# First four experts gathered with the selection matrix stationary, the second-block group moved into mid-stream, stores on two queues

## The chip, the cores and the metric

The kernel runs on one core of a Trainium2 chip. The metric is the device time of one execution in microseconds (us). The unchanged kernel takes 2122.4 us (median of 3 runs, 2119.12 to 2123.26). The core has five engines that run side by side: PE (TensorE, matrix products), DVE (VectorE), ACT (ScalarE), POOL (GpSimd) and SP (SyncE, which here issues most DMAs). In the rows, PEld is PE's loading of the stationary operand.

## The reference, cut to what matters

The program is one layer of one network block and one layer of another, over 512 tokens of width 1024. Nothing is changed in the first three quarters of it. The change is in the last part, a mixture of 64 experts, with two experts for each token:

```python
g_sel = argmax(h2 @ w_rg + b_rg)                  # one of 8 groups of experts
top_v, top_i = top_k(e_logits, 2)                 # two of the 8 experts of that group
gate = p_group * softmax(top_v)
def expert_block(xb, e):
    hid = silu(xb @ w_gate_e[e]) * (xb @ w_up_e[e])     # 1024 -> 256
    return hid @ w_down_e[e]                            # 256 -> 1024
return x + sum over a token's experts of gate * expert_block(h2[token], e)
```

Here `h2` is the normalised sum `x`. Each expert has three float32 matrices of 1 MB, so the weights of the 64 experts are 192 loads of 1 MB.

## The kernel before, in words

**Groups.** Every expert gets a block of 32 slots for tokens, and four experts form a group of 128 slots. `N_Q` is 15: groups 0 to 14 hold four experts each, and group 15 (`H` in the code) holds experts 60 and 61, in 64 slots. Group 16 (`L`) holds the two spare places, experts 62 and 63, each with a first and a *second* block: four blocks of 32 slots for two experts' weights. An expert with more tokens than its slots is put at one of these spare places: `order_prep`, run in groups 1 and 2, permutes the experts from number 24 on, so from there on the load of a weight reads the expert's number from a register (`value_load` in `pump_w`). What is still left over is done in a loop at the very end, whose trip count `nov` is read from memory; the profiled execution doesn't enter it.

**Routing and the first gather** (`ev_out2`, m = 3). The 512 tokens are four tiles of 128 (`m`). For the last tile PE does the transposes of x, the router's logits, and between them the gather of group 0's tokens. That gather is a matrix product with the selection matrix S (`moe["q"][0][1]`, 128 tokens x 128 slots, already scaled by each token's norm): in `gather_quick` the rows of x are the stationary operand, read with a stride of eight columns, and S is streamed, eight products of 128 columns per tile into two PSUM banks, opened by a product with a zero tile (`gather_open`). The result stands transposed (model width on the partitions), so that `gather_last` needs only to scale it by `g8` while it copies it out.

**The order behind it.** DVE picks the two experts per token (`choose`), PE ranks the tokens (`rank`), DVE builds S, PE does the last tile of the gather. Then come `gather_last`, the slots, the index table and the indirect fetch of group 1, the first pair of experts (`pair(0, 0, 0)`), the second pair, the rest of the gates and tables, and `second(0)`.

**A group.** `pair(Q, j, e)` is 32 products (gate and up of two experts, four at a time in column quarters); the trace shows each float32 product as two records, so a pair is 64 records. Between the pairs stand the table and fetch of the next group (`ready`) and the additions of the group before to x (`combine`, products in float32r, then an add on DVE for each half tile). `second` is `hidden`, the 16 products of `down` (32 records), and `group_out`, which splits the result into a high and a low part on ACT and DVE. `turn` transposes the fetched tokens of the next group.

**The weight stream.** `w_order` lists the 192 loads. `pump_w` issues them on SP's queue, in that order, as long as fewer than `N_LIVE` = 13 are live. A load counts as live until the product that uses it is over (`drop_w` in `pair` and `second`). Expert 3 (`E_SMALL`) is loaded in halves into other buffers and isn't counted. `pair(..., last=False)` doesn't drop, so that the spare experts' gate and up serve two pairs.

**The end.** After group 14 come L (its two pairs directly after one another), then H: PE adds x's tiles 1 and 3 into four PSUM banks with an identity product (`sums`, float32), and adds H's result there; tiles 0 and 2 are added on DVE. Eight stores of half a tile go out on SP, in the order of the tiles. Then `nov` is loaded on all engines, the loop is passed over, and the program ends with a DRAIN on each engine.

The lines: L1534 to L1597 `ev_out2` and its tail, L2007 and L2008 `gather_last`, L1857 the weight loads, L113 every product (`mm`), L2292 to L2301 the end, L2366 the end of the program.

Of the kernel before, what the change touches and what calls it, by code (L numbers as in the profile page):

```python
# [12 lines left out]
BF16 = mybir.dt.bfloat16  # L13
# [7 lines left out]
P = 128  # L21
# [57 lines left out]
def layer_kernel(ctx, tc, A, out, dbg=None, stop=None):  # L79
# [1430 lines left out]
    def ev_out2(m, pss):  # L1510
        last = m == NM - 1
        xap = nxt["x"][m]
        xh = halves(xap)
        hT = []

        def tr(b, on_act):
            ps = bank((P, 4, P), "h2T")
            for k in range(4):
                pe.transpose(ps[:, k, :], xap[:, (4 * b + k) * P:(4 * b + k + 1) * P], ident)
            t = m2((P, 4, P), name="h2T")  # L1520
            (act.activation(t, ps, AF.Copy) if on_act else dve.tensor_copy(t, ps))
            hT.append(t)

        def logits():
            lp = bank((P, 96), "lg")
            for k in range(8):
                mm(lp, hT[k // 4][:, k % 4, :], wr[:, k, :], start=k == 0, stop=k == 7)
            return lp

        def biased(lp):  # L1530
            dve.scalar_tensor_tensor(L[:, m, :], lp[:, 0:72], rs_[:, m:m + 1], ro["rbias"], op0=ALU.mult, op1=ALU.add)

        for x_, p_ in zip(xh, pss):
            dve.tensor_tensor(x_, x_, p_, op=ALU.add)  # L1534
        gp.dma_start(x_d[2][m * P:(m + 1) * P, :], xap)
        parts = []

        def rstd_chain(squares):
            return rstd_steps(xh, parts, squares) + [
                lambda: dve.tensor_tensor(rs_[:, m:m + 1], parts[0], parts[1], op=ALU.mult)]  # L1540

        squares = sum_squares(xh)
        if not last:
            steps = rstd_chain(squares)
            if m == 2:
                alternate(steps, rank(0, 2))
            else:
                alternate(steps)
            later(2, lambda: (tr(0, True), tr(1, True)))

            def choice():
                biased(logits())
                if m:
                    alternate(choose(0 if m == 1 else m, m + 1))
            later(3, choice)
            return
        gather_open()
        gather_quick(0, (0, 1))
        tr(0, True)
        tr(1, False)  # L1560
        rk2 = rank(m - 1, m)
        gather_quick(1, (0,))
        lp = logits()
        gather_quick(1, (1,))
        alternate(rstd_chain(squares), rk2)
        gather_quick(2, (0, 1))
        biased(lp)
        alternate(choose(m, m + 1))
        gate_exps()
        alternate(rank(m, m + 1))  # L1570
        gather_quick(3, (0, 1))

    def strided(t, k):

        return t.rearrange("p (i k) -> p k i", k=8)[:, k, :]

    def gather_open():

        moe["gz"] = m2(dt=BF16, name="zero")
        gp.memset(moe["gz"], 0.0)  # L1580
        moe["gps"] = [bank((P, 4, P), "xqT") for _ in range(2)]
        for ps in moe["gps"]:
            mm(ps.rearrange("p k s -> p (k s)"), trb[:, 1, :], moe["gz"], start=True, stop=False)

    def gather_quick(m, bs):

        for b in bs:
            for k in range(4):
                mm(moe["gps"][b][:, k, :], strided(nxt["x"][m], 4 * b + k), moe["q"][0][1][:, m, :],
                   start=False, stop=m == NM - 1 and k == 3)  # L1590

    def gate_exps():

# [270 lines left out]

    N_Q = N_EXP // 4 - 1

    E_SMALL, N_FIRST, N_LIVE = 3, 10, 13
    w_order = []  # L1870
    for e in [*range(0, 4 * N_Q, 2), N_EXP - 2, N_EXP - 4]:
        w_order += [(e + j, i) for j in range(2) for i in range(2)]
        if e >= 4 * N_Q:
            w_order += [(e + j, 2) for j in range(2)]
        elif e % 4:
            w_order += [(e - 2 + j, 2) for j in range(4)]
# [125 lines left out]

    def gather_last():

        xT[0] = [m2((P, 4, P), name="xqT") for _ in range(2)]
        for k in range(4):
            act.activation(xT[0][0][:, k, :], moe["gps"][0][:, k, :], AF.Copy, scale=g8[:, k:k + 1])  # L2007
        dve.tensor_tensor(xT[0][1], moe["gps"][1], g8[:, 4:8, None].to_broadcast([P, 4, P]), op=ALU.mult)  # L2008


    def gate_up(xcs, wts):
# [62 lines left out]
        mm(ps, sel, RkT[0])  # L2074
        dve.tensor_scalar(STs[Q], ps, C("pmod"), None, op0=ALU.is_equal)  # L2075

    def add_group(ps, Q, m, h, start):

        for i, t in enumerate(ys[Q]):
            if Q == N_Q:  # L2080
                r = slice(64 * h, 64 * h + 64)
                mm(ps, STs[Q][r, m * P:(m + 1) * P], t[r, 0], start=start and i == 0, stop=i == 1)
            else:
                mm(ps, STs[Q][:, m * P:(m + 1) * P], t[:, h], start=start and i == 0, stop=i == 1)

    def combine(Q, ms):

# [116 lines left out]
        dve.tensor_copy(ov["key"], p3)  # L2204

    gt_ = gating()
    next(gt_)
    gather_last()
    group_tokens()
    slots(1)  # L2210
    table(1, 4, 6)
    fetch(1)
    for _ in gt_:
        pass
    group_gates()
    sel_S[0] = moe["q"][0][0]
    order, prep = order_prep(), overflow_prep()

# [22 lines left out]
        table(Q)  # L2241
        fetch(Q)

    part = [pair(0, j, j) for j in (0, 2)]
    table(0, 0, 4)
    table(1, 0, 4)
    rank_cols()
# [1 line left out]
    scatter_mat(0)  # L2249
    second(0, hids, range(4))  # L2250
    turn(1)
    for Q in range(1, N_Q):
        part = pair(Q, 0, 4 * Q)
        ready(Q + 1 if Q < N_Q - 1 else Q + 2)
        if Q == N_Q - 2:
            ready(N_Q)
        combine(Q - 1, range(2))
        hids = [hidden(part)]
        part = pair(Q, 2, 4 * Q + 2)
        if Q in (1, 2):  # L2260
            next(order, None)
            next(order, None)
        if Q in (8, 9, 10, 11):
            next(prep, None)
        combine(Q - 1, range(2, NM))
        scatter_mat(Q)
        hids.append(hidden(part))
        turn(Q + 1 if Q < N_Q - 1 else Q + 2)
        second(Q, hids, range(4 * Q, 4 * Q + 4))
    L, H, e = N_Q + 1, N_Q, N_EXP - N_SPARE  # L2270
    part = [pair(L, j, e, last=j > 0) for j in (0, 2)]
    combine(L - 2, range(NM))
    hids = [hidden(p_) for p_ in part]
    scatter_mat(L)
    turn(H)
    second(L, hids, [e, e + 1, e, e + 1])
    scatter_mat(H)
    combine(L, range(NM))

    part = pair(H, 0, 4 * H)  # L2280
    sums = {m: [bank(name="cmb") for _ in range(2)] for m in (1, 3)}
    for m in sums:
        for ps, x_ in zip(sums[m], halves(xt[m])):
            mm(ps, ident, x_, start=True, stop=False)
    hids = [hidden(part)]
    second(H, hids, [4 * H, 4 * H + 1])
    assert wnext["i"] == len(w_order) and not ew and next(order, None) is None and next(prep, None) is None
    for m in range(NM):
        for h, x_ in enumerate(halves(xt[m])):
            if m in sums:  # L2290
                add_group(sums[m][h], H, m, h, False)
                act.activation(x_, sums[m][h], AF.Copy)  # L2292
            else:
                ps = bank(name="cmb")
                add_group(ps, H, m, h, True)
                dve.tensor_tensor(x_, x_, ps, op=ALU.add)
            sp.dma_start(out[0, m * P:(m + 1) * P, h * T:(h + 1) * T], x_)


    nov = nc.values_load(ov["n"][0:1, 0:1], min_val=0, max_val=MAXBLK)  # L2300
    with tc.For_i(0, nov, 1):  # L2301
        ev = sp.value_load(ov["e"][0:1, 0:1], min_val=0, max_val=N_EXP - 1)
        wts = [load_w(i, ev) for i in range(3)]
# [66 lines left out]
```

## Time and profile before

| | |
|---|---|
| median of 3 runs | 2122.4 us (2119.12 to 2123.26) |
| the profiled execution | 2125.34 us, span in the trace 2123.5 us |
| PE busy | 1969.9 us, 93% of the span |
| DVE / ACT / POOL busy | 1127.8 / 752.2 / 103.6 us |
| granted PE clock, mean | 0.959 of full speed |
| HBM read / written | 363.20 MB / 11.10 MB |

In a timeline a row is start, length, engine, line, operation, what it writes and reads, how many records are merged, and in brackets the engine's idle time before it and what ended it. PE's busy time says little here: its matmuls overlap, and their ends are modelled. What matters is which wait ends last, and what the DMA engines move: in the page's 40 slices their rate is 407 to 420 GB/s in slices 32 to 39, the expert part, and far lower before.

### The profile page before, as it was taken

To read this page: it belongs to the slowest core of one execution; us is meant where nothing else is said; L and a number is where in the kernel's file an instruction comes from. 1 tells how busy PE (TensorE), PEld (TensorE's weight loads), DVE (VectorE), ACT (ScalarE), POOL (GpSimd) and SP (SyncE) were. 2 spreads that over 40 slices of the span, in tenths; PEclk is the share of its full clock that TensorE was granted. 3 is DMA by queue.
4 is the path that set the end of the run, shared out by engine and by line. 5 is a ranking of instruction groups with operands and counts; after the bars stand their busy time and mean duration, and the time that the engine had idled before them with its cause. 6 is when DMAs were issued, how large, how long until landed. Compare 5 with 4: busy or idle time off the path is not lost. (4 is left out here: it accounts for less than half of the span.)

```text
span 2123.5 us, 28581 instructions
## 1 busy us (share of the span) xinstructions
PE 1969.9 (93%) x11228; PEld 1480.0 (70%) x11228; DVE 1127.8 (53%) x2447; ACT 752.2 (35%) x1460; POOL 103.6 (5%) x119
## 2 busy tenths in 40 slices
PE   7999999999999999999999999999998887768775
PEld 6777788888888888775678888888876444335433
DVE  5444536436756532878765787766443433343333
ACT  5443323325544422534542654653221211111111
POOL 3000000001000000121110000000000000000000
PEclk9999999999999999999999999999998888888888
DMA  9522222254222262301123332334367999999992
GB/s 223 198 89 68 82 89 72 89 198 139 73 67 80 70 225 92 122 21 28 54 70 109 114 97 90 100 99 119 122 237 274 407 419 419 420 419 420 419 412 115
DMA packets 167193, 369.45 MB, mean 174 GB/s; under 512 B 19033, under 2 KB 117665, under 8 KB 142864
## 3 DMA queue, kind: packets, MB, share of 16 engines
q1 hardware_dynamic: 157536, 341.31, 43.5%
q0 software_dynamic: 9520, 26.28, 4.2%
q8 instruction: 90, 1.47, 0.3%
q14 instruction: 47, 0.39, 0.1%
HBM read 363.20 MB, written 11.10 MB: 176 GB/s over the span
## 5 line engine op out<-in xcount | busy, mean ns | idle before, releaser
L113 PE MATMUL ws<-hTh,wh 128*128 128x512 f32 x1152 | 468.4, 407 | 0.3 <-ACT q2T L1072 0.3
L113 PE MATMUL ws<-hTh,wl 128*128 128x512 f32 x1152 | 450.0, 391 | 0.0
L113 PE MATMUL ws<-hTl,wh 128*128 128x512 f32 x1152 | 449.8, 390 | 0.0
L345 DVE TENSOR_TENSOR wl<-raw,wh 128x1024 fp32r<-128x1024 f32 x230 | 283.9, 1235 | 308.9 <-ACT wh L338 308.1
L338 ACT ACTIVATE wh<-raw 128x1024 fp32r<-128x1024 f32 x247 | 259.0, 1052 | 233.3 <-PE ws L113 106.5
L113 PEld LDWEIGHTS ws<-hTh,wh 128*128 128x128 f32 x1152 | 216.6, 188 | 63.1 <-issue 18.6
L113 PEld LDWEIGHTS ws<-hTh,wl 128*128 128x128 f32 x1152 | 216.6, 188 | 47.0
L113 PEld LDWEIGHTS ws<-hTl,wh 128*128 128x128 f32 x1152 | 217.0, 188 | 43.1 <-issue 2.2
L113 PE MATMUL gu<-we,xT 128*32 128x256 f32 x1984 | 157.5, 434 | 44.7 <-DMA we<-in_w_up_e 30.4
L690 DVE SCALAR_TENSOR_TENSOR cv<-ws,pcol,cv 128x510 f32<-128x510 f32 (+1 forms) x152 | 113.8, 749 | 115.7 <-ACT cv L688 112.5
L113 PEld LDWEIGHTS gu<-we,xT 128*32 128x32 f32 x1984 | 74.7, 124 | 125.8 <-DMA we<-in_w_up_e 42.2
L2092 DVE TENSOR_TENSOR x<-x,cmb 128x512 f32<-128x512 f32 x128 | 79.6, 682 | 60.1 <-PE cmb L113 59.0
L688 ACT ACTIVATE cv<-ws,pcol 128x512 f32<-128x512 f32 x64 | 49.7, 776 | 108.5 <-PE ws L113 108.5
L2018 ACT ACTIVATE part<-gu 128x256 f32<-128x256 f32 x33 | 12.7, 384 | 201.6 <-PE gu L113 201.6
L113 PE MATMUL down<-we,hid 128*32 128x512 f32 x528 | 74.8, 716 | 1.0 <-DVE hid L2031 1.0
L113 PE MATMUL cmb<-ys,ST 128*128 128x512 f32 (+1 forms) x272 | 71.9, 415 | 1.2 <-ACT ys L2055 0.9
L113 PE MATMUL xs<-wh,hTh 128*128 128x512 f32 x160 | 65.9, 412 | 2.1 <-ACT wh L338 2.0
L113 PE MATMUL xs<-wl,hTh 128*128 128x512 f32 x160 | 64.0, 400 | 2.6 <-DVE wl L345 2.6
L2057 DVE SCALAR_TENSOR_TENSOR ys<-down,slot,ys 128x512 fp32r<-128x512 f32 x33 | 24.8, 751 | 76.4 <-ACT ys L2055 76.4
L113 PE MATMUL xs<-wh,hTl 128*128 128x512 f32 x160 | 63.8, 399 | 0.7 <-DVE hTl L307 0.7
L113 PE MATMUL full<-wh,fh 128*128 128x512 f32 x160 | 62.3, 390 | 0.0
L113 PE MATMUL full<-wl,fh 128*128 128x512 f32 x160 | 62.3, 389 | 0.0
(544 smaller groups left out, 3068.1 us busy)
## 6 DMA issues: line engine op xcount, KB each, us to landing
we<-in_w_gate_e SPq DMA_DIRECT2D x63, 1024.0 KB, 19.8
we<-in_w_up_e SPq DMA_DIRECT2D x63, 1024.0 KB, 19.9
we<-in_w_down_e SPq DMA_DIRECT2D x63, 1024.0 KB, 20.1
raw<-in_w_in SPq DMA_DIRECT2D x56, 1024.0 KB, 5.3
raw<-in_w_up SPq DMA_DIRECT2D x22, 1024.0 KB, 5.1
raw<-in_w_down SPq DMA_DIRECT2D x11, 1024.0 KB, 6.1
raw<-in_w_out SPq DMA_DIRECT2D x8, 1024.0 KB, 4.9
AC<-acum_d POOLq DMA_DIRECT2D x16, 512.0 KB, 4.9
```

The source lines that it names most:

```text
L113: pe.matmul(o, l, r, start=start, stop=stop)
L338: act.activation(hi, src, AF.Copy)
L345: eng.tensor_tensor(lo, src, hi.bitcast(F32), op=ALU.subtract)
L688: act.activation(a, src, AF.Identity, scale=taps[0], bias=bias)
L690: dve.scalar_tensor_tensor(a[:, lag:], src[:, :T - lag], taps[lag], a[:, lag:], op0=ALU.mult, op1=ALU.add)
L2018: act.activation(part, gu, AF.Copy)
L2057: dve.scalar_tensor_tensor(lo[:, h], ps, g, hi[:, h].bitcast(F32), op0=ALU.mult, op1=ALU.subtract)
L2092: dve.tensor_tensor(x_, x_, ps, op=ALU.add)
```

## The change

Five things are changed; the diff is cut to their core.

1. The first gather has S stationary and streams x (two products of 512 columns per tile in place of eight of 128). Its result stands with slots on the partitions, so `gather_last` copies it out and transposes it with eight PE transposes before the scaling. The zero tile goes.
2. The slots, table and fetch of group 1, and the rest of the gates, move behind the first pair of group 0 (table and fetch between the two pairs).
3. Group L moves from the end to the place after group 7 (`N_MID` = 8), in the order of the work and in that of the loads, and runs in the loop like any other group. The overflow steps (`prep`) come with groups 9 to 12 in place of 8 to 11.
4. After the last fetch, in group 13, POOL gets a `drain`.
5. At the end x's tiles 1 and 3 take the results of groups 14 and H in PSUM; `nov` is read before H; tiles 1 and 3 are stored whole from ACT's queue, tiles 0 and 2 in halves from SP's, in the order 1, 0, 3, 2.

```diff
-        gather_open()
-        gather_quick(0, (0, 1))
         tr(0, True)
         tr(1, False)
         rk2 = rank(m - 1, m)
-        gather_quick(1, (0,))
+        gather_quick(0)
         lp = logits()
-        gather_quick(1, (1,))
         alternate(rstd_chain(squares), rk2)
-        gather_quick(2, (0, 1))
         biased(lp)
+        gather_quick(1)
+        gather_quick(2)
         alternate(choose(m, m + 1))
         gate_exps()
         alternate(rank(m, m + 1))
-        gather_quick(3, (0, 1))
+        gather_quick(3)
...
+    def gather_quick(m):
+        if m == 0:
+            moe["gps"] = [bank(name="xq") for _ in range(2)]
+        for ps, x_ in zip(moe["gps"], halves(nxt["x"][m])):
+            mm(ps, moe["q"][0][1][:, m, :], x_, start=m == 0, stop=m == NM - 1)
...
-    for e in [*range(0, 4 * N_Q, 2), N_EXP - 2, N_EXP - 4]:
+    N_MID = 8
+    for e in [*range(0, 4 * N_MID, 2), N_EXP - 2, *range(4 * N_MID, 4 * N_Q, 2), N_EXP - 4]:
...
     def gather_last():
+        xq = [m2((P, 4, P), name="xq") for _ in range(2)]
+        for h, ps in enumerate(moe["gps"]):
+            v = ps.rearrange("p (i k) -> p k i", k=8)
+            act.activation(xq[0][:, :, 64 * h:64 * h + 64], v[:, 0:4], AF.Copy)
+            dve.tensor_copy(xq[1][:, :, 64 * h:64 * h + 64], v[:, 4:8])
         xT[0] = [m2((P, 4, P), name="xqT") for _ in range(2)]
-        for k in range(4):
-            act.activation(xT[0][0][:, k, :], moe["gps"][0][:, k, :], AF.Copy, scale=g8[:, k:k + 1])
-        dve.tensor_tensor(xT[0][1], moe["gps"][1], g8[:, 4:8, None].to_broadcast([P, 4, P]), op=ALU.mult)
+        for b in range(2):
+            ps = bank((P, 4, P), "xqT")
+            for k in range(4):
+                pe.transpose(ps[:, k, :], xq[b][:, k, :], ident)
+            if b == 0:
+                dve.tensor_tensor(xT[0][0], ps, g8[:, 0:4, None].to_broadcast([P, 4, P]), op=ALU.mult)
+            else:
+                for k in range(4):
+                    act.activation(xT[0][1][:, k, :], ps[:, k, :], AF.Copy, scale=g8[:, 4 + k:5 + k])
...
-    part = [pair(0, j, j) for j in (0, 2)]
+    part = [pair(0, 0, 0)]
+    slots(1)
+    table(1, 4, 6)
+    fetch(1)
+    part.append(pair(0, 2, 2))
+    for _ in gt_:
+        pass
+    group_gates()
...
+    L, H = N_Q + 1, N_Q
+    seq = [*range(N_MID), L, *range(N_MID, N_Q), H]
+    for i in range(1, len(seq) - 1):
+        Q = seq[i]
+        e = 4 * Q if Q < N_Q else N_EXP - N_SPARE
+        es = [e + j for j in range(4)] if Q < N_Q else [e, e + 1, e, e + 1]
+        part = pair(Q, 0, e, Q < N_Q)
+        if i < len(seq) - 3:
+            ready(seq[i + 1])
+        elif i == len(seq) - 3:
+            ready(seq[i + 1])
+            ready(H)
+            gp.drain()
+        combine(seq[i - 1], range(2))
...
-    L, H, e = N_Q + 1, N_Q, N_EXP - N_SPARE
-    part = [pair(L, j, e, last=j > 0) for j in (0, 2)]
-    combine(L - 2, range(NM))
-    hids = [hidden(p_) for p_ in part]
-    scatter_mat(L)
-    turn(H)
-    second(L, hids, [e, e + 1, e, e + 1])
     scatter_mat(H)
-    combine(L, range(NM))
-    part = pair(H, 0, 4 * H)
     sums = {m: [bank(name="cmb") for _ in range(2)] for m in (1, 3)}
     for m in sums:
         for ps, x_ in zip(sums[m], halves(xt[m])):
             mm(ps, ident, x_, start=True, stop=False)
+    combine(seq[-2], (0, 2))
+    for m in sums:
+        for h in range(2):
+            add_group(sums[m][h], seq[-2], m, h, False, False)
+    nov = nc.values_load(ov["n"][0:1, 0:1], min_val=0, max_val=MAXBLK)
+    part = pair(H, 0, 4 * H)
     hids = [hidden(part)]
     second(H, hids, [4 * H, 4 * H + 1])
-    for m in range(NM):
+    for m in (1, 0, 3, 2):
+        rows = out[0, m * P:(m + 1) * P, :]
         for h, x_ in enumerate(halves(xt[m])):
...
-            sp.dma_start(out[0, m * P:(m + 1) * P, h * T:(h + 1) * T], x_)
-    nov = nc.values_load(ov["n"][0:1, 0:1], min_val=0, max_val=MAXBLK)
+                sp.dma_start(rows[:, h * T:(h + 1) * T], x_)
+        if m in sums:
+            act.dma_start(rows, xt[m])
```

## Rows read from the trace of the kernel before

**Rows 1.** The page, chain of work that ended last, shares of the span by line.
```profile
DMA we<-in_w_up_e 12%; PE gu L113 3%; DMA we<-in_w_down_e 3%; PE cmb L113 1%; PE down L113 1%; PE xqT L113 1%; PE tab L113 0%; DVE x L2092 0%; PE xT L1995 0%; ACT xg L1990 0%; PE ST L113 0%; DVE ov L2167 0%; PE hid L2026 0%; PE lg L113 0%; DVE ST L2075 0%
```
**Rows 2.** Stretches: length, busy of PE, PEld, DVE, ACT, POOL; clock, DMA share, GB/s.
```profile
1595.00:1600.00 5.00, 4.29 (x20) 4.17 (x20) 0.00 (x0) 0.12 (x2) 0.66 (x2) 0.66 0.98 317
...
1609.00:1625.00 16.00, 13.33 (x103) 9.91 (x106) 5.03 (x18) 1.14 (x4) 1.15 (x1) 0.68 0.09 28
...
1625.00:2082.00 457.00, 358.10 (x3113) 194.86 (x3105) 164.65 (x390) 77.89 (x175) 15.05 (x16) 0.85 1.00 412
```
**Rows 3.** Weight loads: first issue after the pause; last issue (last figure), times to landing.
```profile
1624.98 0.33 SPq L1857 DMA_DIRECT2D we<-in_w_gate_e  x1
...
L1857 SPq DMA_DIRECT2D we<-in_w_down_e x4: 333/333/333, 2050.3 to 2067.7; - x4
...
DMA to landing us min/median/max: 19.2/19.7/19.9
```
**Rows 4.** Timeline of the routing of the last tile and the first gather.
```profile
1593.02 1.28 DVE L1534 TENSOR_TENSOR x<-x,full 128x512 f32<-128x512 f32 x2
...
1599.86 1.04 PE L1519 MATMUL h2T<-ca,x 128*128 128x128 f32 x8
...
1602.80 1.92 PE L113 MATMUL lg<-routing,h2T 128*128 128x96 f32 x16
...
1604.56 5.90 PE L113 MATMUL xqT<-S,x 128*128 128x128 f32 x24
...
1608.18 0.23 DVE L1630 TENSOR_TENSOR routing<-rscr,routing 128x64 bf16<-128x64 f32 x1
...
1611.78 4.18 PE L113 MATMUL xqT<-S,x 128*128 128x128 f32 x16 [1.20 <-DVE S L1649]
...
1617.43 1.84 PE L113 MATMUL tab<-routing,S 128*128 128x2 f32 x8 [1.47 <-DVE S L1956]
...
1619.19 3.21 PE L113 MATMUL gu<-we,xqT 128*32 128x256 f32 x28
```
**Rows 5.** PE's timeline of group 3, which waits for no load.
```profile
1696.84 3.63 PE L113 MATMUL gu<-we,xT 128*32 128x256 f32 x64
...
1701.31 2.10 PE L113 MATMUL cmb<-ys,ST 128*128 128x512 f32 x8
...
1720.49 0.60 PE L113 MATMUL gu<-we,xT 128*32 128x256 f32 x6
```
**Rows 6.** Timeline from group 14's second pair to the last addition.
```profile
2047.64 3.64 PE L113 MATMUL gu<-we,xT 128*32 128x256 f32 x58 [1.85 <-DMA we<-in_w_up_e]
...
2058.88 4.38 PE L113 MATMUL down<-we,hid 128*32 128x512 f32 x32
...
2082.95 3.64 PE L113 MATMUL down<-we,hid 128*32 128x512 f32 x32
...
2088.38 0.49 PE L113 MATMUL ST<-RkT,sel 64*128 64x512 f32 x1 [1.79 <-DVE sel L2072]
...
2096.25 3.70 PE L113 MATMUL cmb<-x,ca 128*128 128x512 f32 x8
...
2099.78 0.39 PE L2026 MATMUL hid<-ca,part 128*128 128x128 f32 x2
...
2101.19 1.92 PE L113 MATMUL down<-we,hid 128*32 128x512 f32 x16 [1.01 <-DVE hid L2031]
...
2105.31 2.48 DVE L2296 TENSOR_TENSOR x<-x,cmb 128x512 f32<-128x512 f32 x4 [0.59 <-PE cmb L113]
```
**Rows 7.** Stores and the program's end: durations min/median/max (ns), first and last start (us).
```profile
L2297 SPq DMA_DIRECT2D out<-x x8: 348/406/1553, 2106.0 to 2110.7; - x8
...
DMA to landing us min/median/max: 2.1/4.0/4.4
...
L2366 POOLq DRAIN  x3: 46/103/7173, 2115.5 to 2123.2; - x3
L2366 SPq DRAIN  x3: 7/7/13, 2116.6 to 2122.9; - x3
```

More of the change, by code (lines that the diff above doesn't have):

```diff
@@ L1570, in ev_out2 @@
         alternate(rank(m, m + 1))
-        gather_quick(3, (0, 1))
+        gather_quick(3)
     def strided(t, k):
         return t.rearrange("p (i k) -> p k i", k=8)[:, k, :]
[L1577 to L1587, printed above, removed]
-            for k in range(4):
-                mm(moe["gps"][b][:, k, :], strided(nxt["x"][m], 4 * b + k), moe["q"][0][1][:, m, :],
-                   start=False, stop=m == NM - 1 and k == 3)
+    def gather_quick(m):
[3 more added lines that the diff above has]
+            mm(ps, moe["q"][0][1][:, m, :], x_, start=m == 0, stop=m == NM - 1)
     def gate_exps():
@@ L2003, in gather_last @@
     def gather_last():
-        xT[0] = [m2((P, 4, P), name="xqT") for _ in range(2)]
-        for k in range(4):
-            act.activation(xT[0][0][:, k, :], moe["gps"][0][:, k, :], AF.Copy, scale=g8[:, k:k + 1])
-        dve.tensor_tensor(xT[0][1], moe["gps"][1], g8[:, 4:8, None].to_broadcast([P, 4, P]), op=ALU.mult)
+        xq = [m2((P, 4, P), name="xq") for _ in range(2)]
[3 more added lines that the diff above has]
+            dve.tensor_copy(xq[1][:, :, 64 * h:64 * h + 64], v[:, 4:8])
+        xT[0] = [m2((P, 4, P), name="xqT") for _ in range(2)]
+        for b in range(2):
[7 more added lines that the diff above has]
+                    act.activation(xT[0][1][:, k, :], ps[:, k, :], AF.Copy, scale=g8[:, 4 + k:5 + k])
     def gate_up(xcs, wts):
@@ L2075, in scatter_mat, with add_group @@
         dve.tensor_scalar(STs[Q], ps, C("pmod"), None, op0=ALU.is_equal)
-    def add_group(ps, Q, m, h, start):
+    def add_group(ps, Q, m, h, start, stop=True):
         for i, t in enumerate(ys[Q]):
@@ L2081, in add_group @@
                 r = slice(64 * h, 64 * h + 64)
-                mm(ps, STs[Q][r, m * P:(m + 1) * P], t[r, 0], start=start and i == 0, stop=i == 1)
+                mm(ps, STs[Q][r, m * P:(m + 1) * P], t[r, 0], start=start and i == 0, stop=stop and i == 1)
             else:
-                mm(ps, STs[Q][:, m * P:(m + 1) * P], t[:, h], start=start and i == 0, stop=i == 1)
+                mm(ps, STs[Q][:, m * P:(m + 1) * P], t[:, h], start=start and i == 0, stop=stop and i == 1)
     def combine(Q, ms):
@@ L2206, in layer_kernel @@
     gt_ = gating()
+    gather_last()
     next(gt_)
-    gather_last()
     group_tokens()
[L2210 to L2215, printed above, removed]
     sel_S[0] = moe["q"][0][0]
@@ L2251, in layer_kernel @@
     turn(1)
[L2252 to L2257, printed above, removed]
+    L, H = N_Q + 1, N_Q
[12 more added lines that the diff above has]
+        combine(seq[i - 1], range(2))
         hids = [hidden(part)]
-        part = pair(Q, 2, 4 * Q + 2)
+        part = pair(Q, 2, es[2])
         if Q in (1, 2):
@@ L2262, in layer_kernel @@
             next(order, None)
-        if Q in (8, 9, 10, 11):
+        if Q in (9, 10, 11, 12):
             next(prep, None)
-        combine(Q - 1, range(2, NM))
+        combine(seq[i - 1], range(2, NM))
         scatter_mat(Q)
         hids.append(hidden(part))
-        turn(Q + 1 if Q < N_Q - 1 else Q + 2)
-        second(Q, hids, range(4 * Q, 4 * Q + 4))
-    L, H, e = N_Q + 1, N_Q, N_EXP - N_SPARE
-    part = [pair(L, j, e, last=j > 0) for j in (0, 2)]
-    combine(L - 2, range(NM))
-    hids = [hidden(p_) for p_ in part]
-    scatter_mat(L)
-    turn(H)
-    second(L, hids, [e, e + 1, e, e + 1])
+        turn(seq[i + 1])
+        second(Q, hids, es)
     scatter_mat(H)
-    combine(L, range(NM))
-    part = pair(H, 0, 4 * H)
     sums = {m: [bank(name="cmb") for _ in range(2)] for m in (1, 3)}
```

## The prediction

> **What bounds the kernel now.** I read the chain of waits first. Its largest parts are loads of expert weights, we<-in_w_up_e above all; PE's own parts are small [rows 1]. So in the expert part it is the weight stream that ends last, and PE's work counts only before the stream runs and after it has ended. The windows say the same: from 1625 to 2082 the DMA share is 1.00 at 412 GB/s, but in the 16 us before it is 0.09 [rows 2]. There all 13 live buffers are full, and SP's next load goes out at 1624.98 [rows 3], when the first pair of experts, started at 1619.19, has let its weights go [rows 4]. From there 176 of the 192 loads follow each other without a break. The last is issued at 2067.7 and lands some 19.7 us later [rows 3]: the stream ends at T = 2087.4. With eight loads in flight, 19.7 us to landing is 2.46 us for a load.
>
> Three places are left in which time can be won: the way to the first pair (it shifts the stream, and with it T), the work after T (the last addition ends at 2107.8 [rows 6], 20.4 us later), and the way from there to the end at 2123.5. The sum is made on the span; the profiled execution took 2125.34 us, 2.9 above the median of 2122.4, and I take the same gain off the median.
>
> **Change 1 and 2, the first gather.** x's last tile is complete at 1594.3, the first pair starts at 1619.19 [rows 4]: 24.9 us. Now the new way. A streamed float32 product of 512 columns costs what the identity products of the end cost: 8 records in 3.70 us [rows 6], so 4 records, one tile of the gather, 1.8 us. Before, 24 records of 128 columns took 5.90 and the last 16 took 4.18 [rows 4], about 4 us for a tile. With PE at the upper of its two levels (2.4 GHz; the lower is 1.2):
> - transposes of x: 8 in 1.04 [rows 4], half of them after the second half of x, and three small rank products: to 1595.2;
> - tile 0 of the gather 1.8, logits 1.92 [rows 4]: to 1598.9, where the old logits end at 1604.7;
> - DVE's choice, unchanged, from the old logits' end to 1608.41 [rows 4], 3.7: to 1602.6. Tiles 1 and 2 of the gather (3.6) lie beneath it. Before, the rank products had to wait for the gather until 1610.46 [rows 4];
> - rank to the last S, old 1610.46 to 1611.78 [rows 4], 1.3, then the last tile 1.8: to 1605.7;
> - the new copies, estimated 0.5, four transposes 0.5, the scaling of 128x512 on DVE 0.7 (an addition of that size takes 2.48/4 = 0.6 [rows 6]), and waits 0.2: first pair at 1607.6. The other half of the copies, transposes and scalings lies beside the pair's first half.
>
> That is 11.6 us earlier. The bound below: PE's granted clock was 0.66 in 1595 to 1600 and 0.68 in 1609 to 1625 [rows 2], a mix of its two levels, after idle stretches. At the lower one two uncovered tiles cost 1.8 more each and the transposes 0.5: 7.5 us earlier. I take 10. The moved table takes 1.84 [rows 4] at most; it now stands between the two pairs, so group 0's down weights come free that much later, measured from the first issue. The six loads let go by the pairs cover 6 x 2.46 = 14.8 us and nearly that wait; I cost it 0.5, at most 1.8 if the cover is gone. The zero tile and its products go at no gain beyond this sum. **T moves from 2087.4 to 2077.9.**
>
> **Change 3, group L in mid-stream.** For T it is free if the stream doesn't run dry. A group in which PE waits for nothing takes 1720.49 - 1696.84 = 23.7 us [rows 5]. Twelve loads take 29.5, L's six 14.8, each with a token fetch on top. So in L PE falls back by some 9 us, 3.6 loads; eight are in flight, and the next two groups regain 5.8 each. Cost 0; what hides it is the loads in flight. Bound: 0 to 4 us, if buffers held through L's first pair (which drops nothing) empty the queue. The overflow steps move with their groups; they cost what they did. The loads of 62 and 63 read the order from a register that is written in group 2, well before.
>
> After T the work is now that of group 14 and H, not of L and H. Group 14's second pair waits for a load that has ten others behind it instead of sixteen, so it starts at T - 24.6. Before, it started at 2047.64 and its down ended at 2063.3 [rows 6], 15.6 later: T - 9.0. The scatter matrix of H follows 1.8 later (2086.6 to 2088.38 [rows 6], where it waited for DVE) and takes 0.5; the identity products 3.4 [rows 6], the additions of group 14, now half on DVE and half in PSUM, two times 8 records of 2.0 [rows 5]: T + 0.7. H's weights have landed but for one, so its pair runs, 3.6 [rows 5]: T + 4.3. To the start of its down: 1.4 from the hidden transposes [rows 6] and about 0.6 for ACT's copy: T + 6.3. From there to the last addition 2101.19 to 2107.8 [rows 6], 6.6: **T + 12.9, where it was T + 20.4: 7.5 won**. The bound: at the lower PE level two pairs and a down take up to 3.6 to 4.4 us more each, but PE is seldom idle here; 4 to 9. Before H now come register loads of nov on each engine, under a us, beside PE's queue.
>
> **Change 5, the stores.** SP issues eight, the last at 2110.7, 2.9 after the last addition; they land in 4.0 to 4.4 [rows 7], so at 2114.9. Now SP has four, each behind its addition, and ACT two: last issue 0.4 behind the last addition, landing 4.2 to 4.4 later. **2.3 won**, bounds 1 to 2.9.
>
> **Change 4, the drain.** After the stores have landed, POOL's first DRAIN at 2115.5 takes 7.17 us; the next takes 0.10 [rows 7], and everyone waits. The first has all of POOL's descriptor work since the start behind it, the second nothing. So I take it that the length is a debt of that work, paid once; after group 13's fetches POOL has no more. Paid there, nothing waits behind it: POOL's queue holds only the load of nov and the loop. SP's own drain begins at 2116.6 [rows 7], so the end comes at 2117.5 instead of 2123.5 from the same stores: **6.0 won**; bounds 0 and 6.0. The Trainium skill, page "VectorE: DVE Perf Modes", section "The DRAIN you can't avoid", speaks against it: it has the drains of a program's frame at about 12 ns, constant, on all engines, with no debt to pay. Rows 7 agree for SP (7 to 13 ns) and not for POOL (7173 ns). If the frame's drain owes nothing, the 7 us are something at the program's end and stay; that is the first rival.
>
> Sum: 9.5 + 7.5 + 2.3 + 6.0 = 25.3 us. Span 2098.2, this execution 2100.0, median **2097**.
>
> **The rivals.**
> 1. *The last drain stays long.* For it: only one long drain is in the trace, and it stands behind the passing over of a loop. Against it: the 0.10 of the next. The gain falls to 19.3: 2103. Chance 0.22.
> 2. *The stream gives the head start back.* Group 0's downs or L leave the queue dry, or the early pairs at the lower clock eat the gain. For it: clock 0.68 around the first pair; against it: DMA share 1.00 over 457 us although the early groups are as tight as now. Half of 9.5 lost and 2 more in L: 2104. Chance 0.10.
> 3. *Slower: PE becomes the bound behind L.* With PE's backlog after L and its lower level in play (mean clock 0.85 in the stream [rows 2]), a group might take longer than its share of the stream, about 31 us with its fetch, and the backlog is never made good. From 31 on every us counts seven times (groups 8 to 14); the gain of 25.3 is eaten at 31 + 25.3/7 = 34.6 us for a group. At 36 the time is 2097 + 7 x 5 = 2132. For it: 23.7 us is a group at mostly the upper level. Against it: it would need nearly half of PE's work at the lower level with PE never idle, and the falls that I see follow idle time. Chance 0.05.
> 4. *The gather isn't shorter* (the change doesn't do what it says): the additional copies and transposes and a lower clock eat it; T moves by 3 only: 2104. Chance 0.05.
>
> **How the numbers follow.** The forecast as summed has 0.58. Its own range is 2092 to 2102 (front 7.5 to 11.6, tail 4 to 9, not all at one end). Rivals 1, 2 and 4 end at 2103 to 2104, some us to either side, so the range is 2091 to 2106; rival 3 and the outer parts of the others, some two tenths, are outside. About 0.2% (4 us) is what a measurement of this kernel can tell from no change. Rivals 1, 2 and 4 are all faster by more than that; a sum of them (long drain, half the front, part of the tail) could come within it, for which I leave 0.03. Faster 0.92, same 0.03, slower 0.05.
>
> **What would show it.** First pair at about 1609 and first load after the pause at about 1615 (front); landings without a gap around L and the two groups behind it, share 1.00 (rivals 2 and 3); last weight issue near 2058; from the last landing to the last addition about 13 us with PE busy throughout; last store landing 4.8 behind the last addition; a long POOL DRAIN near group 13 and short ones at the end (else rival 1). The forecast is wrong if the landings show a hole of more than 3 us after L, or if the first pair starts after 1613.

## The result, and the profile after

The changed kernel takes **2100.01 us** (median of 4 runs, 2097.81 to 2102.23), the kernel before beside it 2122.83 (4 runs): ratio 0.9895 [0.9876, 0.9914], 22.8 us less. Forecast were 2097, with a range of 2091 to 2106. The profiled execution took 2101.83 us, its span is 2100.1 (before 2125.34 and 2123.5).

The front first. The timeline of the changed kernel from x's last tile to the first load behind the pause, which answers to [rows 3, 4]:

```profile
1591.27 1.28 DVE L1534 TENSOR_TENSOR x<-x,full 128x512 f32<-128x512 f32 x2
...
1594.98 1.92 PE L113 MATMUL lg<-routing,h2T 128*128 128x96 f32 x16
1596.74 3.62 PE L113 MATMUL xq<-x,S 128*128 128x512 f32 x8
1602.02 1.98 PE L113 MATMUL xq<-x,S 128*128 128x512 f32 x4 [1.20 <-DVE S L1639]
...
1604.48 1.12 PE L2006 MATMUL xqT<-ca,xq 128*128 128x128 f32 x8 [0.47 <-ACT xq L2000]
...
1605.91 3.66 PE L113 MATMUL gu<-we,xqT 128*32 128x256 f32 x64 [0.32 <-DVE xqT L2008]
1609.51 1.05 PE L113 MATMUL tab<-routing,S 128*128 128x2 f32 x8
1609.59 0.33 SPq L1847 DMA_DIRECT2D we<-in_w_gate_e  x1
```

x is complete at 1592.54 (start and length of the first row; the second of its two additions ends there). That is 1.8 us earlier than in [rows 4], but the change doesn't touch what stands ahead of it, and it moves from trace to trace: 1591.0 to 1594.3 in the four traces with the old front, 1589.7 to 1593.5 in the ten with the new one. So times are counted from x below. From there to the first pair it takes 13.4 us where it took 24.9. PE's granted clock in this stretch is 1.00, where it was 0.81; how much of the 11.5 us is the shorter gather and how much the level, no run separates. The pair runs in 3.66 us where its 64 records took 5.76, and the first load goes out 17.0 us behind x instead of 30.7.

Not all of that reaches the end of the stream. Stretches of the changed kernel (columns as in [rows 2]), the whole stream and the place where it fails:

```profile
1610.00:2071.00 461.00, 366.49 (x3161) 196.56 (x3161) 170.91 (x405) 79.91 (x181) 16.20 (x17) 0.85 0.99 410
...
1650.00:1655.00 5.00, 3.60 (x19) 1.85 (x22) 2.01 (x4) 2.45 (x6) 0.00 (x0) 0.75 1.01 423
1655.00:1660.00 5.00, 5.00 (x64) 1.88 (x60) 1.63 (x3) 1.38 (x2) 0.00 (x0) 0.91 0.42 146
```

The share is 1 nearly throughout, around L (1840 to 1920) too, but between 1655 and 1660 it falls to 0.42: 2.9 us of the stream are lost in these five. What stands ahead of the hole is in PE's timeline of group 1:

```profile
1637.38 3.66 PE L113 MATMUL gu<-we,xT 128*32 128x256 f32 x64
...
1644.20 0.27 PE L2125 MATMUL ordT<-ca,ord 128*64 128x128 f32 x1 [2.94 <-DVE ord L2120]
...
1645.18 3.40 PE L113 MATMUL cmb<-ys,ST 128*128 128x512 f32 x8
...
1653.37 4.87 PE L113 MATMUL down<-we,hid 128*32 128x512 f32 x32
```

These are the first steps of the order of experts (`order_prep`): PE waits 2.94 us for DVE, the additions behind them run in 3.40 instead of 2.10 [rows 5], and group 1's down, which lets its loads go, begins 16 us behind the start of the second pair. The kernel before has the same wait, and a smaller hole behind it:

```profile
1655.76 0.27 PE L2122 MATMUL ordT<-ca,ord 128*64 128x128 f32 x1 [2.94 <-DVE ord L2117]
```
```profile
1670.00:1675.00 5.00, 5.00 (x78) 3.08 (x71) 1.71 (x6) 1.07 (x2) 0.00 (x0) 1.00 0.82 308
```

There the share of 0.82 costs 0.9 us, which the mean of 1.00 over 457 us in [rows 2] doesn't let one see. The last weight is issued at 2055.6 and lands 19.7 us later:

```profile
L1847 SPq DMA_DIRECT2D we<-in_w_down_e x1: 333/333/333, 2055.6 to 2055.6; - x1
...
DMA to landing us min/median/max: 19.7/19.7/19.7
```

So the last landing, T, is at 2075.32, against 2087.42.

The end of the timeline, which answers to [rows 6]; the two windows between show the clock:

```profile
2050.54 3.64 PE L113 MATMUL gu<-we,xT 128*32 128x256 f32 x58 [1.30 <-DMA we<-in_w_up_e]
...
2057.55 0.49 PE L113 MATMUL ST<-RkT,sel 64*128 64x512 f32 x1 [1.32 <-DVE sel L2075]
...
2059.88 1.14 PE L1987 MATMUL xT<-ca,xg 64*128 64x64 f32 x8 [1.40 <-ACT xg L1982]
...
2060.95 5.87 PE L113 MATMUL down<-we,hid 128*32 128x512 f32 x32
...
2068.67 0.60 PE L113 MATMUL ST<-RkT,sel 64*128 64x512 f32 x1 [1.85 <-DVE sel L2075]
...
2069.20 5.23 PE L113 MATMUL cmb<-x,ca 128*128 128x512 f32 x8
...
2073.87 4.24 PE L113 MATMUL cmb<-ys,ST 128*128 128x512 f32 x16
...
2078.04 3.66 PE L113 MATMUL gu<-we,xT 128*32 128x256 f32 x64
...
2083.72 1.92 PE L113 MATMUL down<-we,hid 128*32 128x512 f32 x16 [1.01 <-DVE hid L2034]
...
2088.30 2.48 DVE L2306 TENSOR_TENSOR x<-x,cmb 128x512 f32<-128x512 f32 x4 [1.05 <-PE cmb L113]
```
```profile
2060.00:2065.00 5.00, 5.00 (x28) 1.82 (x32) 0.43 (x1) 1.21 (x5) 0.00 (x0) 0.50 0.87 362
2065.00:2070.00 5.00, 3.15 (x18) 1.00 (x11) 2.38 (x5) 1.09 (x2) 0.00 (x0) 0.84 0.47 197
```

The last addition ends at 2090.78, T + 15.5 (T + 20.4 before). H's down starts at 2083.72, 8.4 us behind the last landing: no load is late here, PE is. The identity products take 5.23 us (3.70 in [rows 6]), at a granted clock of 0.70. Group 14's down takes 5.87 us (4.38 in [rows 6]) and ran for most of it at the lower level (clock 0.50 in 2060 to 2065, PE at 1.2 GHz; 0.61 over the whole of the down). Ahead of it stand three gaps of 1.3 to 1.4 us, in which PE waited for a load, DVE and ACT, and PE is idle for 1.85 us again behind it.

Stores and drains, which answer to [rows 7]: SP's stores with their landing, ACT's with theirs, POOL's drain in mid-stream, and the drains at the end.

```profile
L2307 SPq DMA_DIRECT2D out<-x x4: 343/664/1179, 2089.0 to 2091.3; - x4
...
DMA to landing us min/median/max: 3.6/5.7/6.6
...
L2309 ACTq DMA_DIRECT2D out<-x x2: 338/378/418, 2089.0 to 2090.6; - x2
...
L2268 POOLq DRAIN  x1: 13240/13240/13240, 2015.0 to 2015.0; - x1
...
L2377 POOLq DRAIN  x3: 34/47/103, 2098.1 to 2099.8; - x3
L2377 SPq DRAIN  x3: 7/7/13, 2099.2 to 2099.5; - x3
```

The last store is issued 0.5 behind the last addition instead of 2.9, and lands no sooner for it: at 2097.41, 6.6 behind it instead of 7.1. The first drain at the end takes 0.05 us instead of 7.17; the one in mid-stream takes 13.24, and nobody waits for it.

So the terms were, from x: front -10.3, tail -4.9, stores -0.5 (last addition to last landing), drain -5.9 (last landing to the end), together -21.6, and x's own -1.8.

### The profile page after: what moved, and what is told of

Same layout as the page of the kernel before. It is cut to its first block, busy times and chain, and to the rows that moved or that the text cites. A ratio compares the mean times of both kernels' runs of the same rounds, so it can differ in the third digit from the quotient of the medians.

```text
span 2100.1 us, 28491 instructions
## 1 busy us (share of the span) xinstructions
PE 1961.9 (93%) x11186; PEld 1464.9 (70%) x11186; DVE 1126.9 (54%) x2445; ACT 752.4 (36%) x1462; POOL 103.0 (5%) x118
## 5 line engine op out<-in xcount | busy, mean ns | idle before, releaser
L113 PE MATMUL down<-we,hid 128*32 128x512 f32 x528 | 82.1, 766 | 1.0 <-DVE hid L2034 1.0
L113 PE MATMUL full<-wh,fl 128*128 128x512 f32 x160 | 62.2, 389 | 0.0
```

Source lines behind the costliest of these rows:

```text
L113: pe.matmul(o, l, r, start=start, stop=stop)
```

## The experiments

All medians stand beside runs of the kernel before on the same chip. As x's arrival alone moves them by some us, the table takes the segments from each trace; the last column is its span less the last addition. The segments of a row come from one trace. In the rows marked * the landing of the last load isn't in the trace; it is put 2.47 behind that of the load before it, the distance of the last two in the other traces.

| kernel | median, ratio to before | x to first pair | x to T | T to last addition | to the end |
|---|---|---|---|---|---|
| before | 2122.83 | 24.9 | 493.1 | 20.4 | 15.7 |
| changed | 2100.01, 0.9895 [0.9876, 0.9914] | 13.4 | 482.8 | 15.5 | 9.3 |
| changed, again* | 2099.71, 0.9894 [0.9879, 0.991] | 13.4 | 480.0 | 14.9 | 9.3 |
| 1 drain alone | 2116.34, 0.9965 [0.9953, 0.9977] | 24.9 | 493.0 | 20.5 | 9.6 |
| 2 front alone | 2109.48, 0.9937 [0.9923, 0.995] | 13.4 | 482.6 | 20.2 | 14.9 |
| 3 L in mid-stream, sums | 2117.11, 0.9968 [0.9957, 0.9979] | 24.9 | 493.1 | 15.0 | 16.0 |
| 4 order late | 2097.26, 0.9874 [0.9859, 0.9889] | 13.4 | 479.9 | 14.9 | 9.3 |
| 5 table first* | 2100.56, 0.9897 [0.9878, 0.9916] | 16.6 | 482.4 | 15.8 | 9.2 |
| 6 drain early | 2097.94, 0.9882 [0.9865, 0.9898] | 13.4 | 482.5 | 15.5 | 9.3 |
| 7 drain midway | 2118.59, 0.9981 [0.9971, 0.9991] | 25.2 | 494.3 | 20.2 | 12.0 |
| 8 one queue | 2097.5, 0.9884 [0.9867, 0.99] | 13.4 | 480.5 | 15.4 | 8.6 |
| 9 sums early | 2094.46, 0.9867 [0.9846, 0.9888] | 13.4 | 482.6 | 10.2 | 9.3 |
| 10 pair first | 2091.1, 0.9852 [0.9835, 0.9868] | 13.4 | 479.9 | 9.5 | 9.3 |
| 11 no gaps* | 2089.11, 0.9841 [0.9827, 0.9854] | 13.4 | 479.8 | 7.8 | 8.6 |

**1, the drain alone.** The kernel before, with a drain behind its last fetch:

```
         ready(Q + 1 if Q < N_Q - 1 else Q + 2)
         ...
+        if Q == N_Q - 1:
+            gp.drain()
```


> The kernel before, and POOL drains once in group 14's first half, behind the last token fetch. Theory (the first drain behind POOL's descriptor work pays for it once): the drain at the end falls from 7.17 us to some 0.05, last store landing to end from 8.5 us to 2.6, time 2122.8 - 6.0 = 2116.8 us. Rival (the drain at the program's end has a length of its own): 7.2 us at the end as before, time 2122.8 us.

Measured 2116.34. The row of the drains at the end (POOL) in this trace:

```profile
L2368 POOLq DRAIN  x3: 34/47/103, 2114.2 to 2115.9; - x3
```

The longest is 0.10 us, and the end comes 9.6 us behind the last addition instead of 15.7. All other segments are the same to 0.1 us: the 6.1 us are the drain's.

**2 and 3, the front alone and the group alone.** 2 is the kernel before with `gather_quick`, `gather_last` and the order of the first steps of the changed one. 3 has its loop over `seq`, its order of loads and its PSUM sums, with all else as before.

```
 # 2
-    part = [pair(0, j, j) for j in (0, 2)]
+    part = [pair(0, 0, 0)]
+    slots(1); table(1, 4, 6); fetch(1)
+    part.append(pair(0, 2, 2))
 # 3
-    for e in [*range(0, 4 * N_Q, 2), N_EXP - 2, N_EXP - 4]:
+    for e in [*range(0, 4 * N_MID, 2), N_EXP - 2, *range(4 * N_MID, 4 * N_Q, 2), N_EXP - 4]:
```


> The kernel before with the new first gather and the new order of the first steps alone; second blocks, stores and drain as before. In the changed kernel the first weight load after the pause is issued at 1609.6 instead of 1625.0 (x itself is complete 1.8 us earlier, for reasons outside the change), so 13.6 us are the change's; from there to the last landing it takes 465.7 us where the kernel before takes 462.4. Theory (the 3.3 us are lost in groups 0 and 1, where PE cannot let buffers go as fast as the stream fills them): the same 465 to 466 us here, so a gain of 13.6 - 3.3 = 10.3: 2112.5 us (2109 to 2114), with the hole in the DMA share near 1655 to 1660. Rival (they are lost to group L in mid-stream): 462.4 us here, gain 13.6: 2109.2 us, and no hole.

> The kernel before with the group of second blocks behind group 7 and with group 14's results for two tiles added in PSUM; first gather, order of the first steps, stores and the load of the loop count as before, no drain. Theory (free for the stream, and the work behind the last landing is shorter by what the changed kernel shows, 20.4 - 15.5 = 4.9 us): stream length from the first load after the pause to the last landing 462.4 us as before, 2122.8 - 4.9 = 2117.9 us. Rival 1 (the stream runs dry behind L and gives back some 3 us): 465 us, 2121 us. Rival 2 (my forecast's own 7.5 us, the rest lost to something else in the changed kernel): 2115.3 us.

Measured 2109.48 and 2117.11. 2 brings T 10.5 us closer to x, as the changed kernel does (10.3), and has the hole without L being in mid-stream:

```profile
1650.00:1655.00 5.00, 5.00 (x36) 1.54 (x38) 1.42 (x2) 1.83 (x5) 0.00 (x0) 0.76 0.64 262
1655.00:1660.00 5.00, 5.00 (x78) 3.18 (x71) 1.67 (x7) 1.07 (x2) 0.00 (x0) 1.00 0.73 272
```

3 leaves x to T at 493.1 to the tenth: L in mid-stream costs the stream nothing. What it wins behind T is 5.4 us, not 7.5, with nothing else changed. Medians alone would have put 2 on the rival's side (2109.2): in its trace x was complete 4.6 us earlier than in [rows 4].

**4, the order steps later.** The changed kernel, with

```
-        if Q in (1, 2):
+        if Q in (3, 4):
             next(order, None)
             next(order, None)
```


> The changed kernel with the four steps of the order of experts in groups 3 and 4 instead of 1 and 2. In group 1 PE waits 2.9 us for DVE's chain of these steps before its additions, and the loads behind it run dry: DMA share 0.42 in 1655 to 1660. Theory (these waits make the hole): the hole goes, the last landing comes some 2 to 3 us earlier at 2072.5 to 2073.5, time 2097 to 2098 us. Rival (PE's own work in groups 0 and 1 is what is late, the waits fall beside it): the hole stays or moves into group 2, 2100 us.

Measured 2097.26; the same two stretches in its trace:

```profile
1650.00:1655.00 5.00, 5.00 (x32) 1.15 (x28) 0.75 (x1) 1.60 (x5) 0.00 (x0) 0.65 1.01 416
1655.00:1660.00 5.00, 5.00 (x78) 3.18 (x71) 1.65 (x6) 1.07 (x2) 0.00 (x0) 1.00 1.00 388
```

The hole is gone and T is 2.9 us closer to x, so the steps make it. But they don't make the whole of it alone. In the second trace of the changed kernel and in 8, also with the steps in groups 1 and 2, x to T is 480.0 and 480.5 us, and the share falls to 0.83 and 0.76 at the least. In these two PE's clock in 1612 to 1640 was 0.94; in the four traces with the full loss (changed, 2, 6 and 9; 482.5 to 482.8) it was 0.82. In 4, 10 and 11, with the steps moved, it was 0.82 too, and x to T is 479.8 to 479.9. So in these nine traces the full loss goes with both together, the wait for DVE and PE at its lower level more of the time. What sets the clock in these 28 us from one execution to the next, the runs don't show.

**5, the table first.** Kernel 4, with group 1's slots, table, fetch and the gates ahead of the first pair, as before the change:

```
-    part = [pair(0, 0, 0)]
     slots(1)
     ...
     group_gates()
+    part = [pair(0, j, j) for j in (0, 2)]
```


> The kernel with the order steps in groups 3 and 4 (whose stream has no hole behind it: 484.0 us from the last load ahead of the pause to the last landing), with group 1's slots, table and fetch and the gates put back ahead of the first pair, as the kernel before has them. My forecast costed the moved table at 0.5 us behind the first pair, against 1.84 ahead of it. Theory (the way to the first pair sets the stream): first pair 2 to 3 us later, since the gates' part of the chain on DVE has to come first too, and the stream 1.3 to 3 us longer: 485.3 to 487 us, time 2097.3 + 1.3 to 3 = 2098.6 to 2100.3 us. Rival (group 0's second pair and its downs, which come no later, set it): first load later, last landing not, 484.0 us, 2097.3 us.

Measured 2100.56. The first pair starts 3.2 us later and T lies 2.5 us later than in 4. In its timeline the table's own products are the smaller part; PE waits 2.26 us for the selection on DVE, and then runs the pair's 64 records in 4.93 us at clock 0.73 (3.66 at 1.00 in 4); the last row below takes in four more:

```profile
1602.52 1.12 PE L2006 MATMUL xqT<-ca,xq 128*128 128x128 f32 x8 [0.47 <-ACT xq L2000]
1605.89 1.37 PE L113 MATMUL tab<-routing,S 128*128 128x2 f32 x8 [2.26 <-DVE S L1948]
1607.19 5.15 PE L113 MATMUL gu<-we,xqT 128*32 128x256 f32 x68
```

**6 and 7, what the drain owes.** 6 is the changed kernel with the drain in group 2 instead; 7 the kernel before with a drain far ahead of the experts:

```
 # 6
+            if i == 2:
+                gp.drain()
 # 7
                 gp.dma_start(acum_d, t[0:32, :])
+                gp.drain()
```


> The changed kernel with POOL's drain in group 2, behind the fetch for group 3, instead of behind the last fetch; 13 more token fetches follow it. Theory (a debt that grows with POOL's descriptor work since the last drain): the drain at the end is long again, between some 5 us (13 of 16 fetches of the expert part) and 7.17 us, time 2100.0 + 5 to 7 = 2105 to 2107 us. Rival 1 (only the program's first drain on POOL is long, whatever comes after it): 0.05 us at the end, 2100.0 us. Rival 2 (any fetch behind the last drain brings the whole price back): 7.17 us to the hundredth, 2107 us.

> The kernel before, with one POOL drain in the block ahead of the experts, near 1018 us, where POOL has issued 50 of its 87 DMAs; 37 follow, of other kinds and sizes than the token fetches. The two lengths measured at the end (7.17 us behind 87 issues, 1.11 us behind 13) both fit 0.05 us + 0.082 us for each DMA that POOL has issued since its last drain. Theory (a debt by the count of issues): 0.05 + 37 x 0.082 = 3.1 us at the end, time 2122.7 - 4.1 = 2118.6 us. Rival (a debt by bytes or descriptors, of which the 16 token fetches and the loads of the middle block have most or least): by the 13 fetches' share something else, below 2 or above 4 us.

The rows of POOL's drains at the end, of 6 and of 7:

```profile
L2378 POOLq DRAIN  x3: 46/103/1115, 2098.7 to 2100.3; - x3
```
```profile
L2367 POOLq DRAIN  x3: 46/103/3089, 2113.6 to 2117.2; - x3
```

For 6 all three expectations missed the size: 1.11 us. The theory's kind was right and its count wrong: I had divided 7.17 us by the 16 fetches of the expert part, but POOL issues 87 DMAs in the whole program. With 13 behind the last drain, 0.05 + 13 x 0.082 = 1.11; with 87, 0.05 + 87 x 0.082 = 7.18. 7 tested that on 37 issues of other kinds: 3.08 expected by it, 3.09 measured, and the median was 4.3 below the kernel before on its chip where 4.1 was expected. A debt by bytes finds no support: 7's 37 and 6's 13 have one price. In 6 the 1.11 us cost nothing, as SP's own passing over the loop takes as long (to the end 9.3, as in the changed kernel).

**8, the stores on one queue.** The changed kernel, with

```
-                sp.dma_start(rows[:, h * T:(h + 1) * T], x_)
-        if m in sums:
-            act.dma_start(rows, xt[m])
+            sp.dma_start(rows[:, h * T:(h + 1) * T], x_)
```


> The changed kernel with the last result's stores all on SP, as eight halves in the same order of tiles; ACT issues none. Theory (the 2 MB are bound by the transfer, DMA share 1.0 between first and last landing): from the last addition to the last landing 6.6 us as with two queues, to within 0.5, time 2100.0 us. Rival (my forecast's: bound by how late the last store is issued, which one queue does some 2 us later): 8.5 to 9 us, time 2102 us.

Measured 2097.5. Its row of stores and their landing:

```profile
L2307 SPq DMA_DIRECT2D out<-x x8: 343/406/1344, 2084.4 to 2089.4; - x8
...
DMA to landing us min/median/max: 2.0/3.5/4.7
```

The last is issued 2.6 us behind the last addition (2086.72) and lands 6.1 behind it, sooner than with two queues (6.6). From the first issue to the last landing it takes 8.4 us with one queue, 8.5 with two (2088.95 to 2097.41), 8.9 before (8.1 to 9.3 over all traces with those stores). So the last issue doesn't set the end; the times fit an end set by the first issue and the amount. One queue with halves starts its first store earlier, 2.3 instead of 1.8 us ahead of the last addition.

**9 to 11, the tail.** 9 moves the identity products of tiles 1 and 3, and group 13's sums for them, into group 14. 10 is 9 with the order steps of 4, H's scatter matrix ahead of group 14's down, and H's pair ahead of group 14's PSUM sums. 11 is 10 with H's token transposes moved into group 14's first half, so that no gap above 0.2 us is left on PE in the 8 us ahead of group 14's down; it has the sums ahead of H's pair again, and 8's stores; in short:

```
 # 9
+        combine(seq[i - 1], (0,))
+        open_sum(1, seq[i - 1])         # identity product, then group 13's result
 # 11, second half of group 14
+            scatter_mat(Q)
+            hids.append(hidden(part))
+            combine(seq[i - 1], (2,))
+            open_sum(3, seq[i - 1])
+            scatter_mat(H)              # turn(H) already in the first half
         second(Q, hids, es)
```


> The changed kernel with the identity products of tiles 1 and 3 moved into group 14, tile 1 in place of its addition in the first half and tile 3 in the second, and group 13's results for these tiles summed in PSUM too. They took 5.2 us behind group 14's down at PE's lower level, where my forecast had 3.4. Theory (PE is what ends last there, and in group 14 it has gaps of 1.3 to 1.5 us): H's pair starts 4 to 5 us earlier, last landing to last addition 15.5 - 4.5 = 11 us, time 2095.5 us. Rival (the tail hangs on the loads of H's weights, the last of which lands at 2075.3, or on DVE behind group 14): at most 1 us is won, 2099 us.

> The changed kernel with what the runs so far point to, together: order steps in groups 3 and 4 (the run that did that alone had its last landing 2.9 us earlier), identity products in group 14, H's scatter matrix ahead of group 14's down, and H's pair ahead of the PSUM sums of group 14's results, which then lie around its hidden part. Theory (PE bounds the tail until H's down meets the last landing, which leaves 7.1 us behind it): H's down starts some 1 to 2 us behind the last landing, last addition at T + 8 to 9 instead of T + 15.5; time 2100.0 - 2.9 - 7 = 2090 us. Rival (H's pair and down wait for their loads or for DVE, or PE falls to its lower level in the gaps): T + 11 or more, 2093 us or later.

> The changed kernel with order steps in groups 3 and 4, stores as eight halves on SP, and the last two groups put so that PE has no gap ahead of group 14's down: H's token transposes in its first half, in the second half first the scatter matrix and the hidden part, then the remaining additions and identity products, H's scatter matrix, and only then the down; PSUM sums ahead of H's pair. In the run that had the pair ahead of the sums, PE had gaps of 1.4 us ahead of that down, which then ran at the lower level (6.5 us), and the last addition came at T + 9.5. Theory (the gaps cost the level, and H's down can start with the last landing): that down takes about 4 us, last addition at T + 7.5 to 8, time 2091.1 - 1.9 - 0.5 = 2088.7 us. Rival (PE falls to its lower level all the same, or H's pair waits for its loads): T + 9.5, 2091 us.

> The changed kernel as it is, beside the two others on the same chip. Expected of every theory: 2100.0 us within some 2 us.

Measured 2094.46, 2091.1 and 2089.11, beside 2099.71 for the changed kernel again. 9 wins 5.3 us behind T (15.5 to 10.2). In it the identity products and additions alternate on PE; the row behind them is the next operation:

```profile
2045.64 1.02 PE L113 MATMUL cmb<-x,ca 128*128 128x512 f32 x2
...
2048.29 0.39 PE L2029 MATMUL hid<-ca,part 128*128 128x128 f32 x2
...
2059.73 5.34 PE L113 MATMUL down<-we,hid 128*32 128x512 f32 x32
```

From the first identity product of tile 1 to the hidden part it takes 2.65 us, and in that time the tile's four additions in PSUM are done too; in the changed kernel the identity products alone take 2.6 for a tile. In 10 the same down takes 6.46 us at clock 0.56, behind a gap of 1.40 us, in which PE waits for ACT's scaling of H's tokens, and one of 0.27 for DVE:

```profile
2055.84 1.09 PE L1987 MATMUL xT<-ca,xg 64*128 64x64 f32 x8 [1.40 <-ACT xg L1982]
...
2057.92 6.46 PE L113 MATMUL down<-we,hid 128*32 128x512 f32 x32
```

The last addition of 10 comes at T + 9.5, between theory and rival. 11 has the gap elsewhere:

```profile
2055.74 3.64 PE L113 MATMUL down<-we,hid 128*32 128x512 f32 x32
...
2065.15 3.64 PE L113 MATMUL gu<-we,xT 128*32 128x256 f32 x58 [0.28 <-DMA we<-in_w_up_e]
2069.27 0.51 PE L2029 MATMUL hid<-ca,part 128*128 128x128 f32 x2 [0.47 <-ACT part L2021]
2070.78 1.92 PE L113 MATMUL down<-we,hid 128*32 128x512 f32 x16 [1.01 <-DVE hid L2034]
```
```profile
2055.00:2060.00 5.00, 5.00 (x37) 1.42 (x35) 1.50 (x2) 1.18 (x2) 0.00 (x0) 1.00 0.97 403
```

The down takes 3.64 at the upper level (2.4 GHz), H's pair waits for its load, and H's down starts within a us of the last landing (2070.05): T + 7.8, as expected. In the thirteen other traces, all with a gap of 1.40 or 1.41 us close ahead of it, group 14's down took 4.2 to 6.5 us. The gap alone doesn't decide it, though: in the kernel before group 13's down took 3.64 us behind one of 1.41, and in 11 the pair that now follows the gap ran in 3.66. That 11's down is fast because the gap is gone fits all traces of this down, but 11 changes other things as well, and no run moves the gap alone. 10 and 11 also have a small hole one group behind L (share 0.92 and 0.83 in 1910 to 1915); x to T doesn't show it. 11 is the fastest, 10.6 us under the changed kernel on the same chip, 33.5 under the kernel before.

## Why the prediction was right, step by step

The forecast was 25.3 us on the span; measured were 23.4, of which 1.8 are x's. Group L and the drain came out as worked out, tail and stores were put too large, and the front came out by luck in its size.

- **Front, -9.5 forecast, -10.3 measured.** The first pair came 11.5 us earlier, where the sum gave 11.6 and I took 10 for fear of the lower level; PE was at the upper one (granted clock 1.00). The first load came 13.6 earlier, as the pair itself ran in 3.66 us in place of 5.76. Part of rival 2 then happened: of these 13.6 the stream gave back 3.3, of which 2.9 in group 1, by the order steps' wait (4), which the forecast didn't name. The 1.00 over 457 us, which I held against this rival, is a mean; the kernel before has its own hole at these steps (0.82). So the size came out because two errors met, and that is luck. Of the way to the first pair the sum had dropped the table's 1.84 and the 1.47 of waiting ahead of it [rows 4], at a price of 0.5 later: 2.8 net; putting it back cost 2.5 at T (5), and more by the wait for DVE than by the products.
- **L in mid-stream, 0 forecast, 0.0 measured** (3). Rival 3 has nothing for it: in the changed kernel there is no hole behind L, share 1.00 to 1.02.
- **Tail, -7.5 forecast, -4.9 measured.** This is the mis-sized step. I took 3.4 us for the identity products (their own row [rows 6] has 3.70) and had H's pair at T + 0.7. From their start to that of the additions behind them it took 4.7 (their row has 5.23), the scatter matrix came 0.5 later than I had put it, and the pair started at T + 2.7. The last 0.5 is between H's down and the last addition, 7.1 instead of 6.6. I had named the lower level as a bound and set it aside, "PE is seldom idle here". It was idle, for DVE and ACT, ahead of that down and behind it. 9 wins back 5.3 us by doing the identity products ahead of the down, which itself still took 5.34; only 11 has the down at the upper level.
- **Stores, -2.3 forecast, -0.5 measured.** I took the time from issue to landing as fixed and the last issue as what sets the end. The landing times grew from 4.0 to 5.7 us in the median as the issues moved together: the 2 MB take 8.4 to 8.9 us whichever way they are issued (8).
- **Drain, -6.0 forecast, -5.9 measured** (-6.1 alone, in 1). Rival 1 is out. The Trainium skill, page "VectorE: DVE Perf Modes", section "The DRAIN you can't avoid", gives the frame's drains some 12 ns on every engine; SP's agree (7 to 13 ns) and POOL's first one doesn't, in any of the traces with DMAs of POOL behind its last drain (1.11 to 7.17 us).

Rival 4, a gather that isn't shorter, is out with 13.4 against 24.9 us. The low end of the sum's own range, 2092, lies below what all its terms at their best give (11.6 + 9 + 2.9 + 6.0 = 29.5: 2092.9); nothing hangs on it.

## What to carry to other kernels

Where a stream of loads sets the end, count what is won in front of it by the last landing, from a point that the change doesn't touch. The work just behind the first loads, which frees their buffers, has to keep up with the earlier start, or it gives part of it back; look for it in short windows, as a mean over the whole stream hides a hole of some us. Behind the last landing, look for PE's gaps first: they cost their own length, and here often the level of what follows. The stores at the end of this program were worth issuing from the first finished half on, not on more queues.

## What was not expected

- The last drain on POOL takes 0.05 us and 0.082 us for each DMA that POOL issued since its previous drain: 0.05 (none), 1.11 (13), 3.09 (37), 7.17 (87). A drain in mid-stream pays it beside other work; those took 4.73 us (7), 11.74 (6), 12.26 (1) and 13.24 (changed kernel), which is 0.6 (7) and 5 to 6 us more than their counts of some 50, 74 and 87 give; what else they wait for stays open. The three long ones stand right behind a token fetch, the short one behind a plain store.
- The first pair of experts took 3.66 us at granted clock 1.00 in the kernels with the whole of the new front, 4.93 at 0.73 in 5, and 5.76 to 6.04 at 0.63 to 0.60 in those with the old one. Group 14's down took 3.64 us at 1.00 in 11 and 4.2 to 6.5 elsewhere (6.46 at 0.56 in 10), with the same records.
